# Attention heads of a two-layer kernel: order of splits and scores, two scales on ScalarE, residual reads one by one

## The chip, the cores and the metric

The kernel runs on one core of a Trainium2 chip. The metric is device time in microseconds (us) of one execution. Before the change it is 878.94 us, the median of 3 runs (876.65 to 882.01). The core's engines each work through a queue of their own, in program order: TensorE (PE in the profile) for matrix products, VectorE (DVE), ScalarE (ACT), GpSimd (POOL) and SyncE (SP); the last two, and ScalarE at the end, issue transfers. Engines wait for each other by semaphores.

## The reference

Two layers over a sequence of 512 tokens with 1024 features, all in float32. Layer 0 is a state-space mixer, layer 1 an attention with low-rank queries, keys and values (16 heads). The change lies in layer 1:

```python
def mla_mixer(u, positions, in_w, q_norm_w, kv_norm_w, uq_w, ukv_w, out_w):
    proj = u @ in_w                       # c_q 384, c_kv 256, k_r 64, z 2048
    q = (rms_norm(c_q, q_norm_w) @ uq_w)  # 16 heads x (128 + 64 rope)
    kv = (rms_norm(c_kv, kv_norm_w) @ ukv_w)  # 16 heads x (128 keys + 128 values)
    ...
    o = causal_block_attention(q_full, k_full, v, 192 ** -0.5)   # softmax over keys <= query
    o = o.reshape(bsz, seq, 2048) * jax.nn.silu(z)
    return o @ out_w
```

The layer's output is added to the residual stream `h`, and a last RMS norm gives the result.

## The kernel before

**Products in two halves.** To keep float32 accuracy, each operand is split into a rounded part and a remainder, both in the matmul's format: ScalarE casts the first (`whi`, `qh`, `ph`, `va`, `ah`), VectorE subtracts to get the second (`wlo`, `ql`, `pl`, `vb`, `al`). A product is then three matmuls per tile. Weights are loaded by GpSimd's queue into two raw buffers and split on the way (L303, L312).

**Heads.** The attention runs as one loop over 16 heads, `h`, with the work of different heads interleaved. While head `h` has its probabilities multiplied with the values (`product`), the scores of head `h + 1` are computed and turned into probabilities. Queries are taken in 4 blocks `b` of 128; block `b` sees `128 (b + 1)` keys. The steps are:

- `score(h, b)`: five matmuls into a PSUM bank (L871; block 0 is L874 to L876), on VectorE the mask and the row's maximum (L881, L883, called the reduction below), on ScalarE the exponential with its row sum (L257), on VectorE the reciprocal (L889), the scale by it (L890) and a transpose of 32x32 blocks (L892, tile `pb`), then four transfers on SP (L896) that write the block into a scratch tensor `pd` in main memory, so that keys and queries change places.
- `fetch(h)`: four reads on SP (L917), one for each block `kb` of 128 keys, of the turned probabilities into tiles `pl`.
- `turn(h, kb)`: ScalarE casts `pl` to `ph` (L924); VectorE subtracts, in place, so that `pl` is the remainder.
- `product(h, kb)`: three matmuls into the accumulator `po` of the head (L941): `ph` with both halves of the values, and `pl` with the first half. After block 3, VectorE multiplies with `silu(z)` (L943).

**What sets the order.** In this part the order on all engines is the program's own. `sched` runs a feed, a chain of generators that emit the large products and yield a cost in microseconds every six matmuls or so; each yield is a tick. Pieces are placed at a fraction of the feed's total cost, and fire at the first tick whose sum of costs has passed it. The fractions are module constants: `SC` for the four scores of head `h + 1` and its fetch, `TU` for the four turns, `PR` for the four products. An even head's feed is `front_a` (rope, queries and keys of the next pair's first head, cost 5.2) and one product `zgemm` for the gate z (5.2); an odd head's is `front_b` (5.9 with `front_v`, the values), and `zgemm`. From head 11 on, the steps of the output product `out_tok` take the place of `zgemm`. After heads 3, 7 and 11 ScalarE applies silu to four z tiles, which needs another function table before and after.

Work can also be put off: `defer(fn, lag)` puts a function on a list, and each tick counts its lag down; at zero it is emitted, in the order of the list. Before the change, the remainder `pl` has lag 1, the exponential lag 1, the finish of a score (reciprocal, scale, transpose, writes) lag 2, the rope's three VectorE instructions (L742 to L744) lag 3. A consumer that comes earlier calls `now()`. `fetch` calls it for all finishes of its head.

**The output product.** `out_tok(zt, 0, hd)` multiplies the first 8 heads with their weights, in steps of six matmuls for four token blocks `c`, two halves `n` of the features and four weight tiles `u`; four PSUM banks hold the sums of one `n`. The residual was written to the scratch tensor `hd` earlier and is read back into eight tiles `hr` that take the places of finished z tiles, in one go at `n = 0`, `u = 2`, which falls into head 13 (L1101). `done` (L1059) adds the sum.

Of the kernel before, what the change touches and what calls it, by code (L numbers as in the profile page):

```python
# [10 lines left out]
F32 = mybir.dt.float32  # L11
F32R = mybir.dt.float32r
AF = mybir.ActivationFunctionType
ALU = mybir.AluOpType

P = 128
T = 512
D = 1024
KD = D // P
NCH = T // P  # L20
# [20 lines left out]
GN = 16.84  # L41
G7 = 33.0
SF = (0.6, 1.0, 2.0, 3.2, 8.0)
SC = (0.0, 0.1, 0.18, 0.28, 0.55)
TU = (0.08, 0.17, 0.47, 0.57)
PR = (0.35, 0.45, 0.74, 0.94)
ZS = 0.8
KO = (4, 4, 4, 8, 10)
# [114 lines left out]
class Net:  # L163
# [527 lines left out]
    def mla(self):  # L691
        tc, nc, t, wk = self.tc, self.nc, self.t, self.wk
        v = nc.vector
# [6 lines left out]
        hd = self.dram.tile([NCH, P, D], F32, name="hd")  # L700
        turned = hd[:].rearrange("c (j a) d -> a (c j) d", a=32)
        vh, vl = [], []
        for k in range(KD):
            h = self.h[k]
            a = self.act.tile([P, T], F32R, tag="ah", name=self.nm("vh"))
            b = self.act.tile([P, T], F32R, tag="al", name=self.nm("vl"))
# [6 lines left out]
        for i in range(6):  # L713
# [6 lines left out]
            if i >= 2:  # L720
                for k in (2 * i - 4, 2 * i - 3):
                    ht = wk.tile([P, T], F32, tag="ph", name=self.nm("ht"))
                    v.transpose(ht[:], self.h[k][:])
                    for b in range(4):
                        m = slice(32 * b, 32 * b + 32)
# [3 lines left out]
            while pend and i >= NU:  # L729
                o = self.o16.tile([P, T], F32, tag="o", name=self.nm("cq"))  # L730
# [20 lines left out]
        def settle(f):  # L751
            for e in f["w"]:
                e.now()
            f["w"] = []
# [105 lines left out]
        def score(h, b):  # L860
            f, i = F[h // 2], h % 2
            settle(f)
            (qa, qb), kk = f["q", i], f["k", i]
            r = f["r", i]
            n = P * (b + 1)
            s = slice(b * P, (b + 1) * P)
            ps = self.bank("s")
            if b:
                seq = [(qa, kk[:, 0]), (qa, kk[:, 1]), (qb, kk[:, 0]), (r, k1), (r, k2)]
                for k, (x, y) in enumerate(seq):  # L870
                    nc.tensor.matmul(ps[:, :n], x[:, s], y[:, :n], start=k == 0, stop=k == 4)  # L871
            else:
                both = ps[:, :2 * P].rearrange("p (a t) -> p a t", a=2)
                nc.tensor.matmul(both, qa[:, s], kk[:, :, :P], start=True, stop=False)  # L874
                nc.tensor.matmul(ps[:, :P], qb[:, s], kk[:, 0, :P], start=False, stop=False)
                nc.tensor.matmul(both, r[:, s], k12[:, :, :P], start=False, stop=True)  # L876
            p = self.res.tile([P, n], F32, tag="res", name=self.nm("p"))
            st = wk.tile([P, 4], F32, tag="st", name=self.nm("st"), bufs=8)
            mask = self.mask[:, T - n:]
            if b == 0:  # L880
                v.tensor_tensor(p[:], ps[:, P:2 * P], mask, op=ALU.add)  # L881
                mask = p[:]
            v.tensor_tensor_reduce(p[:], ps[:, :n], mask, -SCALE, 3.0e38, ALU.add, ALU.min, st[:, 0:1])  # L883
            p_exp = self.defer(functools.partial(
                self.E, p[:], p[:], AF.Exp, scale=-1.0, bias=st[:, 0:1], accum_out=st[:, 1:2]))

            def finish():
                p_exp.now()
                v.reciprocal(st[:, 2:3], st[:, 1:2])  # L889
                v.tensor_scalar(p[:], p[:], st[:, 2:3], None, op0=ALU.mult)  # L890
                pb = wk.tile([P, T], F32, tag="pb", name=self.nm("pb"))
                v.transpose(pb[:, :n], p[:])  # L892
                turned = pd[h % 2][:].rearrange("(j a) q -> a j q", a=32)
                for i in range(4):
                    q = b * P + 32 * i
                    nc.sync.dma_start(turned[:, :n // 32, q:q + 32],  # L896
                                      pb[32 * i:32 * i + 32, :n].rearrange("a (j q) -> a j q", q=32))

            ends.append(self.defer(finish, 2))

        ends = []
        parts, acc = [[] for _ in range(MH)], {}
# [17 lines left out]
        def turn(h, kb):  # L920
            n = T - kb * P
            pl = back[h, kb]
            ph = wk.tile([P, T], F32R, tag="ph", name=self.nm("ph"))
            nc.scalar.copy(ph[:, :n], pl.bitcast(F32))  # L924
            e = self.defer(functools.partial(
                v.tensor_tensor, pl, pl.bitcast(F32), ph[:, :n].bitcast(F32), op=ALU.subtract))
            parts[h].append((ph, pl, e))

        def product(h, kb):
            f, i, n = F[h // 2], h % 2, T - kb * P  # L930
            if kb == 0:
                acc[h] = self.bank("po")
            po = acc[h]
            settle(f)
            ph, pl, e = parts[h][kb]
            e.now()
            va, vb = f["v"][kb // 2]
            s = slice((kb % 2) * 256 + i * P, (kb % 2) * 256 + (i + 1) * P)
            seq = [(va[:, s], ph[:, :n]), (vb[:, s], ph[:, :n]), (va[:, s], pl[:, :n])]
            for k, (x, y) in enumerate(seq):  # L940
                nc.tensor.matmul(po[:, kb * P:], x, y, start=kb == 0 and k == 0, stop=kb == NCH - 1 and k == 2)  # L941
            if kb == NCH - 1:
                v.tensor_tensor(zt[h][:], po[:], zt[h][:], op=ALU.mult)  # L943
# [25 lines left out]
        def steps(h):  # L969
            return [functools.partial(score, h, b) for b in range(NCH)] + [functools.partial(fetch, h)]  # L970
# [22 lines left out]
        with self.tc.manual_schedule(engines={E.SP, E.DVE, E.Activation, E.Pool}):  # L993
            self.lagging, self.look = True, 2
            self.sched(chain(front_b(0), front_v(0), zgemm(4)), list(zip(SF, steps(0))))
            for h in range(MH):
# [12 lines left out]
                if h % 2 and h < 14:  # L1009
                    feed.append(front_v(j))  # L1010
                at = SC if h + 1 < MH else ()
                pieces = [(x * cost, fn) for x, fn in zip(at, steps(h + 1))]
                pieces += [(x * cost, functools.partial(turn, h, b)) for b, x in enumerate(TU)]
                pieces += [(x * cost, functools.partial(product, h, b)) for b, x in enumerate(PR)]
# [18 lines left out]
    def out_tok(self, o, half, hd):  # L1033
        nc, wk, v, t = self.nc, self.wk, self.nc.vector, self.t
# [10 lines left out]
        def step(ps, c, w, n, ks, start, stop, a=0, b=T):  # L1045
            hi, lo = w
            s = slice(c * P, (c + 1) * P)
            seq = []
            for q, k in enumerate(ks):
                m = slice(q * T + a, q * T + b)  # L1050
                x, y, e = hl[k]
                e.now()
                seq += [(x[:, s], hi[:, m]), (y[:, s], hi[:, m]), (x[:, s], lo[:, m])]
            for i, (x, y) in enumerate(seq):
                nc.tensor.matmul(ps[:, a:b], x, y, start=start and i == 0, stop=stop and i == 5)  # L1055
# [29 lines left out]
        for n in range(2):  # L1085
            last = half == 1 and n == 1
            cuts = [(c, 0, T) for c in range(NCH)]
            if last:
                cuts[-1:] = [(NCH - 1, 0, T // 2), (NCH - 1, T // 2, T)]
            ps = [self.bank("ot") for _ in cuts]  # L1090
            base = U_OUT1 + 8 * half + 4 * n
            for u in range(2 if last else 4):
                w = self.weight("w", base + u)
                self.cut(o, half, 2 * u + 2 + OA)
                if half == 0 and n == 0 and u == 2:
                    for _, _, e in hl:
                        e.now()
                    for c in range(NCH):
                        r = [self.o16.tile([P, T], F32, tag="o", name=self.nm("hr")) for _ in range(2)]
                        for m in range(2):  # L1100
                            nc.sync.dma_start(r[m][:], hd[c, :, m * T:(m + 1) * T])  # L1101
                        self.hh.append(r)
                for q, (c, a, b) in zip(ps, cuts):
                    step(q, c, w, n, (2 * u, 2 * u + 1), u == 0, u == 3, a, b)
                    if b == T:
                        yield 1.3
                    if u == 3:
                        done(q, c, n)
                if half == 0 and n == 1:
                    self.cut(o, 1, 2 * u + 2)  # L1110
            if last:
                w2, w3 = self.weight("w", base + 2), self.weight("w", base + 3)
                for q, (c, a, b) in zip(ps, cuts):
                    step(q, c, w2, n, (4, 5), False, False, a, b)
                    step(q, c, w3, n, (6, 7), False, True, a, b)
                    done(q, c, n, a, b)
                    yield 2.6
# [77 lines left out]
```

## Time and profile before

| | us |
|---|---|
| median of 3 runs | 878.94 |
| the profiled execution | 880.34 |
| its span in the trace | 878.3 |
| TensorE busy | 823.3 (94%) |
| VectorE busy | 674.9 (77%) |
| ScalarE busy | 449.5 (51%) |
| first score to last product of the attention heads | about 480 to 822 |

A row of a timeline gives the start in us from the span's beginning, the length, the engine, the line, the instruction, what it writes and reads, its shape, and in brackets how long the engine sat idle before it and which instruction released it. A row of the waits gives who waited for whom, the total in us, how often, and the longest. A row of stretches gives the stretch, its length, busy time and count for PE, PEld (weight loads of TensorE), DVE, ACT and POOL, the clock granted to TensorE (1.00 is full speed), the DMA share and GB/s. A row of groups gives the number of instructions, their busy time in us and the mean in ns, then the idle time before them.

### The profile page before, as it was taken

To read this page: it belongs to the slowest core of one execution; us is meant where nothing else is said; L and a number is where in the kernel's file an instruction comes from. 1 tells how busy PE (TensorE), PEld (TensorE's weight loads), DVE (VectorE), ACT (ScalarE), POOL (GpSimd) and SP (SyncE) were. 2 spreads that over 40 slices of the span, in tenths; PEclk is the share of its full clock that TensorE was granted. 3 is DMA by queue.
4 is the path that set the end of the run, shared out by engine and by line. 5 is a ranking of instruction groups with operands and counts; after the bars stand their busy time and mean duration, and the time that the engine had idled before them with its cause. 6 is when DMAs were issued, how large, how long until landed. Compare 5 with 4: busy or idle time off the path is not lost.

```text
span 878.3 us, 11881 instructions
## 1 busy us (share of the span) xinstructions
PE 823.3 (94%) x4068; PEld 688.0 (78%) x4068; DVE 674.9 (77%) x1298; ACT 449.5 (51%) x794; POOL 50.5 (6%) x100
## 2 busy tenths in 40 slices
PE   7999999999999999999999979998988988878995
PEld 5887888888888888888887858786876877766885
DVE  7889898888888798775768867878786877856544
ACT  7566665646465565343535534464446456523333
POOL 0000000000000000000102110110101011000000
PEclk9999999999999999999999998998999999998998
DMA  6363542524333243236532455555555545475222
GB/s 226 110 189 109 166 144 97 167 73 145 104 128 128 97 144 96 108 98 142 141 100 61 115 128 130 154 138 123 133 132 138 147 115 130 127 226 133 72 72 96
DMA packets 144492, 111.57 MB, mean 127 GB/s; under 512 B 108592, under 2 KB 116272, under 8 KB 144432
## 3 DMA queue, kind: packets, MB, share of 16 engines
q1 hardware_dynamic: 134944, 79.61, 32.3%
q0 software_dynamic: 8768, 30.15, 11.6%
q10 hardware_dynamic: 720, 1.05, 0.3%
q8 instruction: 32, 0.52, 0.2%
q14 instruction: 28, 0.23, 0.1%
HBM read 93.60 MB, written 14.81 MB: 123 GB/s over the span
## 4 chain that ended last, share of the span: by engine, by line
PE 62%; DVE 16%; DMA 11%; SPq 4%; ACT 4%; issue 3%; DVEq 0%; POOL 0%; ACTq 0%
PE mm L332 41%; PE ot L1055 6%; DMA pd<-pb 5%; PE mm L341 4%; SPq L896 3%; DMA pl<-pd 3%; DVE wlo L63 2%; PE yd L149 2%; PE po L941 2%; DVE pb L892 1%; DVE p L890 1%; PE yd L332 1%; PE aux L141 1%; PE s L871 1%; PE aux L116 1%
## 5 line engine op out<-in xcount | busy, mean ns | idle before, releaser
L312 ACT CAST whi<-raw 128x1024 fp32r<-128x1024 f32 (+3 forms) x132 | 126.8, 965 | 194.0 <-PE mm L332 167.9
L63 DVE TENSOR_TENSOR wlo<-raw,whi 128x1024 fp32r<-128x1024 f32 (+3 forms) x132 | 146.4, 1113 | 42.2 <-ACT whi L312 42.1
L332 PE MATMUL mm<-ah,whi 128*128 128x512 f32 x384 | 153.8, 401 | 0.0
L332 PE MATMUL mm<-ah,wlo 128*128 128x512 f32 x384 | 150.1, 391 | 0.4 <-DVE wlo L63 0.4
L332 PE MATMUL mm<-al,whi 128*128 128x512 f32 x384 | 149.8, 390 | 0.0
L332 PE MATMUL mm<-vh,wlo 128*128 128x512 f32 x224 | 89.8, 401 | 1.2 <-DVE wlo L63 1.2
L332 PE MATMUL mm<-vh,whi 128*128 128x512 f32 x224 | 89.9, 401 | 0.6 <-ACT whi L312 0.6
L332 PE MATMUL mm<-vl,whi 128*128 128x512 f32 x224 | 89.1, 398 | 0.0
L332 PEld LDWEIGHTS mm<-ah,wlo 128*128 128x128 f32 x384 | 72.1, 188 | 16.1 <-DVE wlo L63 0.8
L332 PEld LDWEIGHTS mm<-ah,whi 128*128 128x128 f32 x384 | 72.1, 188 | 15.4 <-issue 1.4
L332 PEld LDWEIGHTS mm<-al,whi 128*128 128x128 f32 x384 | 72.2, 188 | 14.5 <-DVE al L353 0.3
L303 POOL DMA_DIRECT2D raw<-in_w_dram x36 | 19.2, 534 | 629.9 <-DMA hd<-ht 417.7
L924 ACT CAST ph<-pl 128x512 fp32r<-128x512 f32 (+1 forms) x64 | 27.8, 454 | 52.9 <-DMA pl<-pd 42.4
L1055 PE MATMUL ot<-whi,ah 128*128 128x512 f32 (+1 forms) x136 | 53.0, 389 | 0.0
L1055 PE MATMUL ot<-wlo,ah 128*128 128x512 f32 (+1 forms) x136 | 52.8, 388 | 0.0
L1055 PE MATMUL ot<-whi,al 128*128 128x512 f32 (+1 forms) x136 | 52.8, 388 | 0.0
L257 ACT ACTIVATE p<-p,st 128x128 f32<-128x128 f32 (+1 forms) x64 | 35.8, 560 | 32.7 <-DVE st L883 32.6
L332 PEld LDWEIGHTS mm<-vh,wlo 128*128 128x128 f32 x224 | 43.0, 192 | 11.7 <-DVE wlo L63 2.1
L332 PEld LDWEIGHTS mm<-vh,whi 128*128 128x128 f32 x224 | 43.0, 192 | 9.2 <-ACT whi L312 0.8
L63 DVE TENSOR_TENSOR pl<-pl,ph 128x512 fp32r<-128x512 f32 (+1 forms) x64 | 30.0, 481 | 25.7 <-ACT ph L924 25.7
L332 PEld LDWEIGHTS mm<-vl,whi 128*128 128x128 f32 x224 | 43.1, 192 | 8.1
L941 PE MATMUL po<-pl,va 128*128 128x512 f32 (+1 forms) x64 | 23.9, 374 | 24.3 <-DVE pl L63 24.3
(228 smaller groups left out, 1746.0 us busy)
## 6 DMA issues: line engine op xcount, KB each, us to landing
raw<-in_w_dram SPq DMA_DIRECT2D x64, 512.0 KB, 3.3
raw<-in_w_dram POOLq DMA_DIRECT2D x36, 512.0 KB, 3.7
L<-ac_d SPq DMA_DIRECT2D x32, 256.0 KB, 3.9
E<-ea_d SPq DMA_DIRECT2D x32, 128.0 KB, 3.4
raw<-in_ua_dram POOLq DMA_DIRECT2D x8, 512.0 KB, 3.9
pd<-pb SPq DMA_DIRECT2D x64, 64.0 KB, 2.0
pl<-pd SPq DMA_DIRECT2D x16, 256.0 KB, 2.7
pd<-pb SPq DMA_DIRECT2D x64, 48.0 KB, 1.8
```

The lines of the kernel that those rows point to most:

```text
L63: self.fn()
L116: nc.tensor.matmul(pp[c], self.BT[:, c * P:(c + 1) * P], flat(self.xw[:, c]), start=True, stop=True)
L149: nc.tensor.matmul(yd[64 * h:64 * h + 64, s], self.xdt[j][:, c, h, :], self.L[2 * j + h][:, s], start=True, stop=True)
L257: i = self.nc.scalar.activation(out, in_, func, **k)
L303: self.wqueue.dma_start(raw[:], self.t[kind][idx])
L312: nc.scalar.copy(hi[:, a:b], raw[:, a:b])
L332: self.nc.tensor.matmul(ps, a, b, start=i == 0, stop=i == len(seq) - 1)
L341: self.nc.tensor.matmul(p, seq[i][0], seq[i][1], start=i == 0, stop=i == 3 * ks - 1)
L896: nc.sync.dma_start(turned[:, :n // 32, q:q + 32], pb[32 * i:32 * i + 32, :n].rearrange("a (j q) -> a j q", q=32))
L924: nc.scalar.copy(ph[:, :n], pl.bitcast(F32))
L941: nc.tensor.matmul(po[:, kb * P:], x, y, start=kb == 0 and k == 0, stop=kb == NCH - 1 and k == 2)
L1055: nc.tensor.matmul(ps[:, a:b], x, y, start=start and i == 0, stop=stop and i == 5)
```

## The change

Five things are edited.

1. The fractions: scores at 0, 0.06, 0.14, 0.22 (before 0, 0.1, 0.18, 0.28), the fetch at 0.6 (0.55); turns at 0.18, 0.25, 0.46, 0.57 (before 0.08, 0.17, 0.47, 0.57).
2. `turn` emits the remainder `pl` at once behind the cast `ph`, instead of one tick later.
3. The finish of a score is cut in two: `even` (reciprocal and scale) with lag 2, and the transpose and writes with lag 3 for blocks 2 and 3, lag 2 for blocks 0 and 1.
4. For blocks 2 and 3 the scale is an activation (copy with a scale per partition) on ScalarE instead of VectorE's `tensor_scalar`.
5. The residual's eight reads are issued one by one ahead of the steps of `out_tok`: four in `n = 0`, `u = 2` (head 13), four in `n = 1`, `u = 0` (head 14).

```diff
-SC = (0.0, 0.1, 0.18, 0.28, 0.55)
-TU = (0.08, 0.17, 0.47, 0.57)
+SC = (0.0, 0.06, 0.14, 0.22, 0.6)
+TU = (0.18, 0.25, 0.46, 0.57)
...
-            def finish():
+            def even():
                 p_exp.now()
                 v.reciprocal(st[:, 2:3], st[:, 1:2])
-                v.tensor_scalar(p[:], p[:], st[:, 2:3], None, op0=ALU.mult)
+                if b > 1:
+                    nc.scalar.activation(p[:], p[:], AF.Copy, scale=st[:, 2:3])
+                else:
+                    v.tensor_scalar(p[:], p[:], st[:, 2:3], None, op0=ALU.mult)
+
+            p_even = self.defer(even, 2)
+
+            def finish():
+                p_even.now()
                 pb = wk.tile([P, T], F32, tag="pb", name=self.nm("pb"))
                 v.transpose(pb[:, :n], p[:])
...
-            ends.append(self.defer(finish, 2))
+            ends.append(self.defer(finish, 3 if b > 1 else 2))
...
             nc.scalar.copy(ph[:, :n], pl.bitcast(F32))
-            e = self.defer(functools.partial(
-                v.tensor_tensor, pl, pl.bitcast(F32), ph[:, :n].bitcast(F32), op=ALU.subtract))
-            parts[h].append((ph, pl, e))
+            v.tensor_tensor(pl, pl.bitcast(F32), ph[:, :n].bitcast(F32), op=ALU.subtract)
+            parts[h].append((ph, pl))
...
-                if half == 0 and n == 0 and u == 2:
+                fresh = half == 0 and u == (0 if n else 2)
+                if fresh:
                     for _, _, e in hl:
                         e.now()
-                    for c in range(NCH):
-                        r = [self.o16.tile([P, T], F32, tag="o", name=self.nm("hr")) for _ in range(2)]
-                        for m in range(2):
-                            nc.sync.dma_start(r[m][:], hd[c, :, m * T:(m + 1) * T])
-                        self.hh.append(r)
                 for q, (c, a, b) in zip(ps, cuts):
+                    if fresh:
+                        r = self.o16.tile([P, T], F32, tag="o", name=self.nm("hr"))
+                        nc.sync.dma_start(r[:], hd[c, :, n * T:(n + 1) * T])
+                        if n == 0:
+                            self.hh.append([])
+                        self.hh[c].append(r)
                     step(q, c, w, n, (2 * u, 2 * u + 1), u == 0, u == 3, a, b)
```

More of the change, by code (lines that the diff above doesn't have):

```diff
@@ L934, in product @@
             settle(f)
-            ph, pl, e = parts[h][kb]
-            e.now()
+            ph, pl = parts[h][kb]
             va, vb = f["v"][kb // 2]
```

## Prediction

> **What bounds the kernel now.** I read the page first, then TensorE's waits, the granted clock by stretches, and the timelines of a few heads. The page: TensorE (PE) is busy 94% of the span, so what can be won is mostly where it stands still:
>
> ```profile
> span 878.3 us, 11881 instructions
> PE 823.3 (94%) x4068; PEld 688.0 (78%) x4068; DVE 674.9 (77%) x1298; ACT 449.5 (51%) x794; POOL 50.5 (6%) x100
> ```
>
> The waits of PE between 480 and 822 us, the stretch of the attention heads (total, times, longest), hold nearly all of that:
>
> ```profile
> PE po L941 <- DVE pl L63: 24.3, 10, 4.6
> PE po L941 <- ACT ph L924: 9.2, 3, 5.0
> PE s L871 <- DVE vb L63: 2.9, 1, 2.9
> PE s L874 <- DVE k L63: 0.8, 1, 0.8
> PE mm L332 <- DVE wlo L63: 0.7, 1, 0.7
> ```
>
> Sum: 37.9 us. The first two rows, 33.5 us, are products (L941) that wait for the split of the probabilities: `ph` on ScalarE (ACT), `pl` on VectorE (DVE). A stall also costs afterwards. Two stalls from PE's timeline, and then the stretches (length, busy us of PE, PEld, DVE, ACT, POOL, then clock, DMA share, GB/s); 560 to 568 and 714 to 722 are those of the two stalls:
>
> ```profile
> 564.07 0.39 PE L941 MATMUL po<-pl,va 128*128 128x256 f32 x1 [2.02 <-DVE pl L63]
> ...
> 715.42 0.39 PE L941 MATMUL po<-pl,va 128*128 128x256 f32 x1 [2.27 <-DVE pl L63]
> ```
>
> ```profile
> 480.00:822.00 342.00, 303.90 (x1461) 256.32 (x1460) 252.77 (x585) 165.25 (x344) 40.17 (x77) 0.94 0.53 135
> 560.00:568.00 8.00, 5.98 (x32) 4.95 (x32) 6.24 (x10) 1.85 (x3) 0.54 (x1) 1.00 0.57 122
> 598.00:610.00 12.00, 8.75 (x33) 7.31 (x34) 8.53 (x18) 3.44 (x8) 1.07 (x2) 0.72 0.56 135
> 714.00:722.00 8.00, 6.58 (x28) 5.60 (x29) 5.43 (x11) 4.56 (x8) 0.00 (x0) 0.79 0.59 164
> 738.00:746.00 8.00, 5.37 (x21) 4.75 (x22) 4.50 (x14) 4.85 (x10) 1.40 (x3) 0.79 0.50 148
> ...
> 682.17:698.60 16.43, 16.43 (x93) 14.45 (x93) 15.34 (x36) 7.67 (x18) 1.60 (x3) 1.00 0.55 132
> ```
>
> 342 x (1 - 0.94) = 20.5 us of clock were withheld. Each patch takes 1.7 us (8 x 0.21) or 3.4 us (12 x 0.28); some 3 us of the sum fell into the stalls themselves, so 17.5 us come on top. The last row is head 9, which has no stall: 16.4 us, and a pair of heads at full pace takes about 32. **To be won at most: 37.9 + 17.5 = 55.4 us.**
>
> Why is `pl` late? ACT's largest wait of these 342 us, then head 6 in the timelines of DVE, ACT and PE (start, length, and in brackets the idle time before):
>
> ```profile
> ACT ph L924 <- DMA pl<-pd: 42.4, 10, 10.3
> ```
>
> ```profile
> 627.71 0.69 DVE L63 TENSOR_TENSOR pl<-pl,ph 128x512 fp32r<-128x512 f32 x1 [1.80 <-ACT ph L924]
> ...
> 636.27 1.18 DVE L63 TENSOR_TENSOR wlo<-raw,whi 128x1024 fp32r<-128x1024 f32 x1
> 637.38 0.68 DVE L742 TENSOR_TENSOR rraw<-rraw,con 128x512 f32<-128x512 f32 x1
> ...
> 639.30 0.62 DVE L63 TENSOR_TENSOR pl<-pl,ph 128x256 fp32r<-128x256 f32 x2
> ...
> 627.05 0.62 ACT L924 CAST ph<-pl 128x512 fp32r<-128x512 f32 x1 [3.46 <-DMA pl<-pd]
> 634.17 0.60 ACT L924 CAST ph<-pl 128x256 fp32r<-128x256 f32 x2
> ...
> 639.77 0.38 PE L941 MATMUL po<-pl,va 128*128 128x256 f32 x1 [3.04 <-DVE pl L63]
> ```
>
> `ph` of block 2 was ready at 634.5. Its `pl`, deferred by one tick, stood behind a weight's `wlo` and the rope (637.38 to 639.30, 1.92 us), and DVE worked without a gap: it was late, because ACT had sat 3.46 us on the first `ph` of the head, with the exponentials of the next head queued behind it.
>
> **The change, part by part.** In even heads the cost of the feed is 5.2 + 5.2 = 10.4, and pieces fire at the first tick past fraction x cost.
>
> (1) `pl` right behind `ph`. For block 2 it comes ahead of the rope: 1.92 us earlier. Nothing is added; but DVE now stops there if `ph` is late.
>
> (2) Turn 0 goes from the tick at 1.30 to that at 2.79. The exponentials of the next head's blocks 0 to 2 now stand ahead of `ph` 0, so ACT's 3.46 us and DVE's 1.80 us of idle are filled. Score 3 comes before the second half of the q gemm. The fetch (0.55 to 0.6) stays at the tick past 6.24, that is 6.88; it only has to stay behind the later finish.
>
> (3) Scale of blocks 2 and 3 on ACT:
>
> ```profile
> L890 DVE TENSOR_SCALAR p<-p,st 128x512 f32<-128x512 f32 x16 | 7.8, 487 | 0.6
> L890 DVE TENSOR_SCALAR p<-p,st 128x384 f32<-128x384 f32 x16 | 6.8, 427 | 0.6
> L1080 ACT ACTIVATE hr<-hr,ss x4: 722/724/725, 863.9 to 873.9; 128x512 f32<-128x512 f32 x4
> L251 ACT ACT_TABLE_LOAD  x12: 1283/1283/1283, 55.2 to 738.0; - x12
> ```
>
> DVE loses 0.49 + 0.43 = 0.91 us a head. L1080 is the same operation (copy with a scale per partition): 0.72 us for 512 columns; for 384 I take 0.62, between 0.43 (DVE's) and 0.72. L1080 ran beside exponentials, after the last table load at 738.0, so no load is added. ACT gains 1.34 us a head: 165 + 16 x 1.34 = 187 of 342 us, cover enough, but the scale is one more hand-over DVE - ACT - DVE ahead of the transpose.
>
> Together in head 6. Block 3's transpose ends where `wlo` starts, at 636.27; without 1.80 of idle and 0.91 of scales, and with 0.3 for ACT's hand-overs, at 633.9. `pl` 2 starts at 639.30 now; 1.80 + 0.91 + 1.92 = 4.6 us earlier is 634.7, and since block 3's exponential now waits behind block 2's scale (0.62) I put 0.7 on it: 635.4, done at 635.8. PE wants it at 639.77 - 3.04 = 636.7. **No stall, but a slack of only 0.9 us**; the longest stall of this kind, 4.6, is just covered too.
>
> Odd heads have no stall now; there `pl` 0 goes behind a k remainder and two reductions. Head 9:
>
> ```profile
> 686.23 0.69 DVE L63 TENSOR_TENSOR pl<-pl,ph 128x512 fp32r<-128x512 f32 x1
> ...
> 689.67 0.54 DVE L883 CUSTOM_DVE_ANT_0 p<-s,con 128x384 f32<-128x384 f32 x1
> ...
> 690.50 0.39 PE L941 MATMUL po<-pl,va 128*128 128x512 f32 x1
> ```
>
> Without `pl` the reduction starts at 689.1, `pl` follows and ends at 690.2: slack 0.3 us. Transposes 2 and 3 now come as a pair after `pl` 2, ending some 1 us later than now, and their eight writes fill SP's queue together, so the fetch goes some 1.7 us later; even heads want their `ph` 0 late enough to bear that by some 1.7 us.
>
> (4) The residual's reads. Eight reads stood between two pairs of head 14's writes (SP and the chain of waits), and both last heads stalled on the fetch:
>
> ```profile
> 770.96 3.95 SPq L1101 DMA_DIRECT2D hr<-hd  x8
> 773.41 6.03 DMA hr<-hd
> 789.62 0.79 PE L941 MATMUL po<-ph,va 128*128 128x512 f32 x1 [5.02 <-ACT ph L924]
> 810.63 0.50 PE L941 MATMUL po<-ph,va 128*128 128x512 f32 x1 [2.99 <-ACT ph L924]
> ```
>
> Three remain ahead of those writes, 3/8 of 6.03 = 2.3 us: 3.8 us earlier; also the exponentials of head 15 no longer queue behind `ph` of head 14. Of the other four, one goes ahead of head 15's last writes. I leave 1 us of the 5.02 and, with its clock, 3 us in head 15.
>
> **What stays of the 55.4 us.** The waits for k and wlo at the start, 1.5; head 0's first product, whose fetch isn't moved, 9.2 - 5.0 - 3.0 = 1.2; the tail, 4. After heads 3, 7 and 11 ACT loads tables for silu and DVE stands still:
>
> ```profile
> 587.16 0.69 DVE L63 TENSOR_TENSOR vb<-mm,va 128x512 fp32r<-128x512 f32 x1 [4.72 <-ACT va L852]
> ...
> 589.98 0.69 DVE L63 TENSOR_TENSOR pl<-pl,ph 128x512 fp32r<-128x512 f32 x1
> ...
> 591.21 0.39 PE L941 MATMUL po<-ph,va 128*128 128x512 f32 x1
> ```
>
> In head 4 the third reduction (0.54), its exponential (0.81), `ph` (0.62) and `pl` (0.69) now follow 589.98: `pl` at 592.8 where PE wants it at 591.7, and some 0.9 us again at block 2: 2 us each in heads 4 and 8, 4 together. Head 12's wait for `vb` (2.9 us, clock 1.2) hangs on the same silu and isn't touched: 4.1. The other eleven heads at 0.3, for slacks this thin: 3.3. Sum 18.1, gain 55.4 - 18.1 = 37.3 us. The profiled execution took 880.34 us (span 878.3, 2.0 around it), 1.4 above the median of 878.94: 880.3 - 37.3 - 1.4 = 841.6, **842 us**.
>
> One rule of the Trainium skill bears on the clock's part: "TensorE: Matmul & The Clock Gate", Part 1, has the clock halved only after a whole idle window of about 3.4 us. The trace differs: the stretch 714 to 722, clock 0.79, follows a stall of 2.27 us; the one with 1.00 followed 2.02 us. By the page head 12 and head 15 would keep 1 to 2 us less, 840 us; I go by the rows.
>
> **Rivals.** (a) The hand-over becomes the wait: `pl` 0, its slack 0.3 us in odd heads, or transpose 2 behind ACT's scale comes 1.5 us late in each of 15 heads, 22 us: 864 us. For it: ACT stands between two steps of DVE four times a head. Against it: ACT has the room.
> (b) The tail and heads 4, 8 and 12 come free too, since all before them is earlier: 842 - 12 = 830 us (4 + 4 + 4.1). Against it: the silu and its table loads stay where they are.
> (c) It doesn't do what it says: DVE, with 252.77 - 14.6 = 238 us of work in 305, cannot close its gaps, and each stall moves to the next remainder: 878 us.
> (d) Slower: the loop fetch - `ph` 0 - exponential 3 - transpose 3 - write - fetch becomes the bound. Landing, min/median/max, of the writes (L896) and of the fetch (L917):
>
> ```profile
> L896 SPq DMA_DIRECT2D pd<-pb x256: 302/449/1698, 496.9 to 800.5; - x128
> ...
> DMA to landing us min/median/max: 1.4/1.8/6.1
> ...
> DMA to landing us min/median/max: 2.5/3.0/4.2
> ```
>
> With the medians a lap of an even head is 6.1 us from `ph` 0 to the last transpose (627.8, behind the exponential of block 2, to 633.9 above), four issues of 0.45, 1.8 to land, an issue and 3.0 for the fetch: 13.1 us. In an odd head the `ph`, `pl`, reductions and `wlo` in front of two transposes make 7.2 us, and seven issues wait in a row: 15.6. Together 28.7, under PE's 32. At the maxima it is 28.7 + 2 x (4.3 + 1.2) = 39.7, or 7.7 over PE's 32 in each of 7 pairs: 842 + 54 = 896 us. It passes PE's pace once write and fetch together land 1.7 us late in each head, and the present time once they land some 4.3 us late. Against it: medians far below.
>
> **How the numbers follow.** Forecast 0.57 (832 to 853), (a) 0.17, (b) 0.12, (c) 0.06, (d) 0.08. Faster by over 0.5% (4.4 us, about what a measurement tells from no change): 0.57 + 0.17 + 0.12 = 0.86; same 0.06; slower 0.08. The range 828 to 868 leaves out (c), (d) and the ends of (a) and (b).
>
> **What would show it.** Right: in PE's waits `po <- pl` falls from 24.3 to under 5 us; the clock over the heads rises to 0.98; ACT's wait `ph <- DMA pl` drops from 42 us; the stall at head 14's first product is about 1 us; head 12's wait for `vb` stays. (a) shows as `po` waiting for `pl` or `ph` of 512 columns, (d) as ACT's `ph` waiting for the fetch in even heads, and (c) as DVE busy over 90% there. The forecast is wrong if waits of PE beyond 20 us remain between the first score and the last product.

## The result and the profile after

The changed kernel took **854.11 us** (median of 4 runs, 853.53 to 857.82) against 877.8 us of the kernel before beside it: ratio **0.973, 95% interval 0.969 to 0.978**. It is faster, as forecast, and inside the range (828 to 868), but the gain is 24 us where 37 were worked out. The profiled execution took 854.5 us, its span 852.5.

From the page after, the span and the busy times, with the instructions of each engine:

```profile
span 852.5 us, 11895 instructions
PE 815.8 (96%) x4068; PEld 678.7 (80%) x4068; DVE 660.1 (77%) x1266; ACT 468.6 (55%) x826; POOL 50.9 (6%) x100
```

DVE lost 32 instructions and ACT gained 32: the scales of two blocks in 16 heads. The waits of PE, and one of ACT's, between 480 and 822 us (total, times, longest):

```profile
PE po L947 <- DVE pl L933: 8.1, 17, 1.5
PE po L947 <- ACT ph L932: 8.0, 6, 3.9
PE s L871 <- DVE vb L63: 2.9, 1, 2.9
PE s L874 <- DVE k L63: 0.8, 1, 0.8
PE mm L332 <- DVE wlo L63: 0.7, 1, 0.7
...
ACT ph L932 <- DMA pl<-pd: 19.4, 9, 7.8
```

37.9 us of waits have become 20.5, but in 26 places instead of 16. ACT's wait for the fetch, 42.4 us before, was to go in the even heads; 19.4 us of it stay, 11.7 of them in heads 14 and 15. The granted clock, in the same stretch of 342 us and in the two places where it is still low (length, busy time of PE, PEld, DVE, ACT, POOL, then clock, DMA share, GB/s):

```profile
480.00:822.00 342.00, 321.03 (x1573) 267.44 (x1573) 249.04 (x570) 190.78 (x385) 43.00 (x82) 0.99 0.56 143
...
720.00:728.00 8.00, 6.51 (x20) 5.74 (x21) 4.89 (x17) 4.35 (x12) 2.59 (x5) 0.57 0.45 120
784.00:790.00 6.00, 5.18 (x15) 3.98 (x16) 4.20 (x7) 3.63 (x7) 0.53 (x1) 0.72 0.77 241
```

Withheld there: 8 x 0.43 = 3.4 us and 6 x 0.28 = 1.7 us, together 5.1. So 20.5 + 5.1 = **25.6 us stay of what the prediction put at 55.4; it had left 18.1.** In a second profile of the same kernel (run 11 below) the waits are 22.9 us. Five stalls from PE's timeline show which kinds are left (start, length, matmul, and in brackets how long PE stood still and for whom):

```profile
625.82 0.39 PE L947 MATMUL po<-pl,va 128*128 128x256 f32 x1 [0.79 <-DVE pl L933]
...
708.08 0.50 PE L947 MATMUL po<-pl,va 128*128 128x512 f32 x1 [1.52 <-DVE pl L933]
721.49 0.80 PE L871 MATMUL s<-k,qh 128*128 128x256 f32 x2 [2.94 <-DVE vb L63]
764.86 0.50 PE L947 MATMUL po<-ph,va 128*128 128x512 f32 x1 [1.70 <-ACT ph L932]
784.82 0.50 PE L947 MATMUL po<-ph,va 128*128 128x512 f32 x1 [3.93 <-ACT ph L932]
```

The first is head 6; heads 0, 2, 4, 8 and 10 stall at the same product by 0.79 or 0.80 us. Then head 11 at product 0, the wait for `vb` of head 12, and the first products of heads 14 and 15.

**Head 6, where the prediction had "no stall, but a slack of only 0.9 us".** SP's queue from the end of head 5 (start, time over which the transfers were issued, count), then the chain of waits over the same time (start, length, what; a `DMA` row runs from the start of the issue to the landing):

```profile
602.44 8.95 SPq L904 DMA_DIRECT2D pd<-pb  x9
```

```profile
609.20 1.67 SPq L904
...
610.90 4.12 DMA pd<-pb
615.09 2.96 DMA pl<-pd
```

The last of head 5's writes is out at 602.44 + 8.95 = 611.39, and the fetch has to wait until it has landed: 610.90 + 4.12 = 615.02, so it leaves at 615.09. The timelines of PE, ACT and DVE around it:

```profile
610.08 0.27 PE L947 MATMUL po<-pl,va 128*128 128x128 f32 x1
...
624.75 0.28 PE L947 MATMUL po<-ph,vb 128*128 128x256 f32 x1
...
618.13 0.62 ACT L932 CAST ph<-pl 128x512 fp32r<-128x512 f32 x1 [2.48 <-DMA pl<-pd]
...
605.32 0.43 DVE L933 TENSOR_TENSOR pl<-pl,ph 128x256 fp32r<-128x256 f32 x1 [1.53 <-ACT ph L932]
605.66 1.16 DVE L900 STREAM_TRANSPOSE pb<-p 128x384 f32<-128x384 f32 x2
...
618.78 0.69 DVE L933 TENSOR_TENSOR pl<-pl,ph 128x512 fp32r<-128x512 f32 x1 [2.22 <-ACT ph L932]
...
624.20 1.23 DVE L63 TENSOR_TENSOR wlo<-raw,whi 128x1024 fp32r<-128x1024 f32 x1 [0.22 <-ACT whi L312]
```

The pair of transposes stands behind `pl` 2 of head 5, for which DVE waited 1.53 us: its `ph` stood on ACT behind the two scales (603.76 to 604.99). The fetch leaves 5.0 us after head 5's last matmul (610.08). Before, that matmul started at 622.36 and the fetch left 1.6 us behind it (timelines of SP, DVE and PE):

```profile
611.11 9.56 SPq L896 DMA_DIRECT2D pd<-pb  x16
623.97 1.86 SPq L917 DMA_DIRECT2D pl<-pd  x4
...
617.01 0.71 DVE L892 STREAM_TRANSPOSE pb<-p 128x512 f32<-128x512 f32 x1
...
622.36 0.27 PE L941 MATMUL po<-pl,va 128*128 128x128 f32 x1
```

So DVE still stands 2.22 us idle on the first `ph`, as before (1.80), although three exponentials now go ahead of it, and `pl` 2 is late again, behind a weight's `wlo`, though only by 0.79 us instead of 3.04.

### The profile page after: what moved, and what is told of

Its sections match the earlier page's. It is cut to its first block, busy times and chain, and to the rows that moved or that the text cites. A ratio compares the mean times of both kernels' runs of the same rounds, so it can differ in the third digit from the quotient of the medians.

```text
span 852.5 us, 11895 instructions
## 1 busy us (share of the span) xinstructions
PE 815.8 (96%) x4068; PEld 678.7 (80%) x4068; DVE 660.1 (77%) x1266; ACT 468.6 (55%) x826; POOL 50.9 (6%) x100
## 3 DMA queue, kind: packets, MB, share of 16 engines
q0 software_dynamic: 8768, 30.15, 11.7%
## 4 chain that ended last, share of the span: by engine, by line
PE 62%; DVE 13%; DMA 10%; ACT 7%; issue 4%; SPq 4%; DVEq 0%; POOL 0%; ACTq 0%
PE mm L332 40%; PE ot L1061 7%; DMA pd<-pb 4%; PE mm L341 4%; DMA pl<-pd 3%; SPq L904 3%; PE yd L149 2%; DVE wlo L63 2%; PE s L871 2%; ACT whi L312 2%; PE yd L332 1%; PE aux L141 1%; DVE pl L933 1%; PE po L947 1%; PE aux L116 1%
## 5 line engine op out<-in xcount | busy, mean ns | idle before, releaser
L332 PE MATMUL mm<-vh,wlo 128*128 128x512 f32 x224 | 87.7, 392 | 1.2 <-DVE wlo L63 1.2
L332 PE MATMUL mm<-vl,whi 128*128 128x512 f32 x224 | 87.3, 390 | 0.0
L332 PE MATMUL mm<-ch,whi 128*128 128x512 f32 x104 | 42.1, 405 | 0.0
L332 PE MATMUL mm<-cl,whi 128*128 128x512 f32 x104 | 41.3, 397 | 0.0
```

What stands on the lines that cost most here:

```text
L332: self.nc.tensor.matmul(ps, a, b, start=i == 0, stop=i == len(seq) - 1)
```

## The experiments

The first four are each one part of the change on the kernel before; the cut of the finish with its later lag and the scale on ScalarE count as one part, and no run separates them.

**1. The remainder alone.**

```diff
-            e = self.defer(functools.partial(v.tensor_tensor, pl, ...))
+            v.tensor_tensor(pl, pl.bitcast(F32), ph[:, :n].bitcast(F32), op=ALU.subtract)
```

> The kernel before with one edit: the remainder pl is emitted at once behind its cast ph. Theory A (the rope was the wait): pl 2 of each even head comes 1.92 us earlier on VectorE, so the nine stalls shrink from 24.3 us to about 9, with two or three patches of slow clock fewer: 860 us. Theory B (ScalarE, blocked on the fetch, was the wait): turn 0 still stands ahead of the next head's exponentials, VectorE now waits for ph sooner, and what the rope gives back is lost there: 872 us or more.

Measured: 871.3 us, ratio 0.996 (0.993 to 0.998). From the waits of PE and of ACT:

```profile
PE po L939 <- DVE pl L925: 15.7, 13, 2.7
PE po L939 <- ACT ph L924: 11.5, 5, 6.1
...
ACT ph L924 <- DMA pl<-pd: 65.7, 14, 10.2
```

`po` waits less for `pl`, and more for `ph`; ACT's wait for the fetch grows from 42.4 to 65.7 us. The remainder was not late by its place in the queue alone.

**2. The order alone.**

```diff
-SC = (0.0, 0.1, 0.18, 0.28, 0.55)
-TU = (0.08, 0.17, 0.47, 0.57)
+SC = (0.0, 0.06, 0.14, 0.22, 0.6)
+TU = (0.18, 0.25, 0.46, 0.57)
```

> The kernel before with the new fractions alone (scores, fetch and turns). Theory A: pl 2 still stands behind the rope, so the stalls of even heads stay near 2 us each: 868 us. Theory B: ScalarE and VectorE no longer idle on the first ph (3.5 and 1.8 us a head), and most of the gain of the whole change is here: 860 us or less.

Measured: 872.5 us, ratio 0.994 (0.992 to 0.997). Waits of PE and ACT, and a stall from PE's timeline:

```profile
PE po L941 <- DVE pl L63: 27.6, 18, 4.7
...
ACT ph L924 <- DMA pl<-pd: 5.3, 2, 4.4
```

```profile
554.98 0.50 PE L941 MATMUL po<-pl,va 128*128 128x512 f32 x1 [1.74 <-DVE pl L63]
```

The later turns do what the second part of the change was to do: ACT's wait for the fetch falls to 5.3 us. Yet ACT now stands 31.6 us at the same casts until PE's products release it (1.8 us before), and with `pl` still one tick behind `ph`, `po` now waits for `pl` at product 0 too (554.98). Neither theory had that.

**3 and 4. The scale on ScalarE alone, and the residual's reads one by one alone.**

```diff
-                v.tensor_scalar(p[:], p[:], st[:, 2:3], None, op0=ALU.mult)
+                if b > 1:
+                    nc.scalar.activation(p[:], p[:], AF.Copy, scale=st[:, 2:3])
...
+            p_even = self.defer(even, 2)
...
-            ends.append(self.defer(finish, 2))
+            ends.append(self.defer(finish, 3 if b > 1 else 2))
```

```diff
-                if half == 0 and n == 0 and u == 2:
+                fresh = half == 0 and u == (0 if n else 2)
...
```

> The kernel before with the finish cut in two and the scale of blocks 2 and 3 on ScalarE alone. Relief of VectorE (0.91 us a head) would give about 5 us: 873 us. The rival, the lap through memory: transposes 2 and 3 come one tick later, so the writes and the fetch come later and ScalarE sits longer on the first ph: no gain, 878 to 890 us.

> The kernel before with the residual's reads one by one alone. If the eight reads held up head 14's writes: the stall there falls from 5.0 to 1 or 2 us and loses a patch of slow clock: 873 us. If head 14's fetch was late by its scores anyway: 878 us.

Measured: 878.4 us, ratio 1.000 (0.997 to 1.002), and 877.5 us, ratio 1.000 (0.998 to 1.003). With the scale on ACT, ACT's wait for the fetch is 56.9 us instead of 42.4; with the single reads head 14's stall is 2.07 us instead of 5.02, as wanted, but the waits for `pl` are 27.9 us instead of 24.3. By itself neither part can be told from no change. The four parts alone add up to 11 us (6.4 + 5.3 - 0.7 + 0.3 = 11.3); the whole change gave 24.

**5. The changed kernel without the scale on ScalarE** (scale on VectorE, lag 2, as before).

> The changed kernel with the scale of blocks 2 and 3 back on VectorE and one finish of lag 2: order, pl and reads together. Theory A (order and pl open the way together, VectorE's relief of 0.91 us a head still counts, since even heads stall 0.8 us at pl 2 in the changed kernel): each even head loses 0.9 us more, 862 us. Theory B (the pair of transposes in odd heads and the hand-over to ScalarE cost what the relief brings, as the scale alone gave nothing): 852 to 856 us, with the fetch of even heads some 2 us earlier in the head.

Measured: 851.2 us, ratio 0.970 (0.966 to 0.974): not slower than the changed kernel; the 3 us by which it is faster are not clear of noise, since the intervals overlap. The end of head 14 in SP's timeline and the first product of head 15, here and then in the changed kernel:

```profile
766.61 8.10 SPq L896 DMA_DIRECT2D pd<-pb  x16
...
778.27 1.80 SPq L917 DMA_DIRECT2D pl<-pd  x4
...
781.68 0.50 PE L939 MATMUL po<-ph,va 128*128 128x512 f32 x1
```

```profile
772.64 5.16 SPq L904 DMA_DIRECT2D pd<-pb  x8
780.57 2.01 SPq L925 DMA_DIRECT2D pl<-pd  x4
```

Without the scale on ACT the last writes are out at 774.71, the fetch of head 15 leaves at 778.27 and its product doesn't wait; with it the last eight writes are out at 777.80, the fetch leaves at 780.57, and PE waits 3.93 us. That isn't all gain: in kernel 5 head 14 stalls 2.19 and 1.55 us (1.70 and 0.55 in the changed kernel), so the last two heads together wait 3.7 us instead of 6.2. And head 4 stalls 2.37 us at `pl` 2 instead of 0.80: there the relief of VectorE was worth something. All waits of PE between 480 and 822 us are 19.8 us, against 20.5 and, in run 11, 22.9.

**6. The scale on ScalarE only where it is emitted in even heads** (that is, for the scores of odd heads; lag 2 for the others).

```diff
-                if b > 1:
+                if b > 1 and h % 2:
...
-            ends.append(self.defer(finish, 3 if b > 1 else 2))
+            ends.append(self.defer(finish, 3 if b > 1 and h % 2 else 2))
```

> The changed kernel with ScalarE's scale and lag 3 kept in even heads only; in odd heads blocks 2 and 3 are finished as before (VectorE, lag 2), ahead of pl 2. If the lap through memory makes the stalls of 0.8 + 0.2 us in even heads (ScalarE waits 2.5 us for the fetch there, whose writes came as a pair late in the odd head), the fetch comes 1 to 2 us earlier, these stalls vanish, and the time is 846 us. If VectorE's work is the cause: odd heads get 0.91 us more, 855 to 858 us.

Measured: 851.2 us, ratio 0.969 (0.966 to 0.973). Head 6 in the timelines of SP, PE, ACT, DVE and PE:

```profile
604.45 4.15 SPq L904 DMA_DIRECT2D pd<-pb  x8
612.21 1.77 SPq L925 DMA_DIRECT2D pl<-pd  x4
...
609.77 0.27 PE L947 MATMUL po<-pl,va 128*128 128x128 f32 x1
...
615.24 1.02 ACT L932 CAST ph<-pl 128x512 fp32r<-128x512 f32 x2
...
616.17 0.65 DVE L933 TENSOR_TENSOR pl<-pl,ph 128x512 fp32r<-128x512 f32 x1
...
623.83 0.28 PE L947 MATMUL po<-ph,vb 128*128 128x256 f32 x1
623.95 0.28 PE L947 MATMUL po<-pl,va 128*128 128x256 f32 x1
```

Here the odd head's writes end at 608.6, the fetch leaves 2.4 us after head 5's last matmul instead of 5.0, neither ACT nor DVE waits for it, and the 0.79 us at `pl` 2 are gone, in heads 2 and 10 too. What the loop emits in head 6 is the same in both kernels; only head 5's part differs. And kernels 5 and 9, which also finish head 6's scores on VectorE, have the fetch at +1.5 and +2.3 us and no stall at `pl` 2 of head 6. **That the late fetch makes this stall is shown**, for head 6 best; head 2's is no steady sign (0.25 us in run 11, 0.84 in kernel 5). Head 15, whose scores still have their scale on ACT, keeps its stall (3.94 us). That the scale in the even heads helps is not shown: with it (851.15) and without it (851.21) the time is the same. The 846 us expected were not reached: heads 0, 4, 8, 11, 12 and 14 keep stalls of about the old size.

**7 and 8. The silu in heads 4, 8 and 12** instead of 3, 7 and 11, on the changed kernel and on kernel 6.

```diff
-                if h < 13 and h % 4 == 3:
-                    pieces.append((ZS * cost, functools.partial(zsilu, h // 4 + 1)))
+                if h in (4, 8, 12):
+                    pieces.append((ZS * cost, functools.partial(zsilu, h // 4)))
```

> The changed kernel with the three groups of silu one head later, in heads 4, 8 and 12 instead of 3, 7 and 11, where no value's remainder waits behind them. If head 12's wait for vb (2.9 us, and 3.4 us of clock) and the 0.75 us at the first products of heads 4 and 8 hang on the silu's place on ScalarE: 8 us less, 846 us. If ScalarE's 4.8 us only hit the next head's exponentials instead: 852 to 856 us, with stalls in heads 5, 9 and 13.

> The two edits before this one together. If both causes hold and are independent: 838 to 840 us, all that my forecast left out for even heads and head 12. If they share the same slack: no better than the better one of them.

Measured: 861.2 us, ratio 0.981 (0.978 to 0.985), and 854.8 us, ratio 0.975 (0.971 to 0.979): each slower than the same kernel with the silu in its old place, by 5 to 7 us on the changed kernel (its intervals just touch) and by 3.7 us on kernel 6. A stall of kernel 7 from PE's timeline, in head 5, where the changed kernel has none:

```profile
601.11 0.50 PE L947 MATMUL po<-ph,va 128*128 128x512 f32 x1 [1.59 <-ACT ph L932]
```

The wait for `vb` (2.9 us) is gone. In its place heads 5 and 9 wait 1.6 and 1.5 us each at product 0, a score waits 1.9 us at 748.74, and all waits of PE grow from 20.5 to 23.2 us.

**9 and 11. The order and the remainder together on the kernel before** (edits 1 and 2), and beside it the changed kernel once more.

> The kernel before with two parts of the change, pl right behind ph and the new order; the scale stays with VectorE and the eight reads stay together. Alone these two gave 6.5 us (871.3 against 877.7) and 5.4 us (872.5). Theory A: they only work together, because the new order brings the wait of pl at product 0 (which lagged one tick behind the remainders) and pl alone leaves ScalarE's wait on the fetch (65.7 us); together they carry all but the last two heads: 851 to 855 us, pl waits near 11 us as in the run without the scale, and the stall of head 14's first product back at 3 to 5 us. Theory B: the single reads carry a part of their own (alone they were worth nothing, since the stall of head 14 was then taken by pl): 857 to 861 us, with 4 us or more in heads 14 and 15 alone.

> The changed kernel itself, beside the other two on one chip: 852 to 856 us. Theory A (the two parts order and pl carry the gain): within 2 us of e9_order_and_pl. Theory B (the reads carry a part, the scale none): 3 us or more below it.

Measured: 857.2 us, ratio 0.976 (0.973 to 0.979), and 856.3 us, ratio 0.976 (0.973 to 0.979). **Two of the four parts together give as much as the whole change; alone they gave 6.4 and 5.3 us, together 21.** The other two together are worth 0.9 us, which can't be told from nothing. But it need not be nothing twice. Kernel 5 is kernel 9 with the single reads, and its ratio, 0.970, is lower. First product of head 14 in PE's timeline, and the stretch of the last heads, of kernel 9:

```profile
770.88 0.79 PE L939 MATMUL po<-ph,va 128*128 128x512 f32 x1 [6.31 <-ACT ph L924]
```

```profile
757.00:797.00 40.00, 32.63 (x140) 26.32 (x140) 20.90 (x45) 13.54 (x27) 2.11 (x4) 0.87 0.60 173
```

and of kernel 5:

```profile
763.50 0.50 PE L939 MATMUL po<-ph,va 128*128 128x512 f32 x1 [2.19 <-ACT ph L924]
```

```profile
757.00:797.00 40.00, 36.17 (x156) 28.83 (x155) 25.09 (x53) 15.31 (x29) 2.64 (x5) 0.96 0.56 169
```

The stall is 4.1 us shorter and the clock withholds 40 x 0.09 = 3.6 us less: by the medians the reads are worth some 6 us (857.2 to 851.2), and the scale on ACT then takes 3 to 5 of them back (851.2 to 854.1 or 856.3). Kernels 5 and 9 were not run side by side, and the intervals just touch or overlap, so these two sizes are not shown; of the traces' part the shorter stall is firm, the clock less so (last section).

**10 and 12. The silu at the end of heads 3, 7 and 11**, behind both casts of `va`, on kernel 6 and on kernel 5.

```diff
-                    pieces.append((ZS * cost, functools.partial(zsilu, h // 4 + 1)))
+                    pieces.append((2 * cost, functools.partial(zsilu, h // 4 + 1)))
```

> The changed kernel with ScalarE's scale only in even heads (851.2 us before) and with the silu of heads 3, 7 and 11 put at the end of these heads, behind both casts of va, so that VectorE's vb no longer waits for the silu and its table loads. Theory A: the wait for vb at head 12 (2.9 us, and 3.4 us of withheld clock behind it) goes, and the first exponentials of the next head bear the silu's 4.8 us: 845 to 847 us, and the VectorE wait for va falls from 18.5 us to under 8. Theory B: the silu then stands ahead of the first exponentials and the first ph of heads 4, 8 and 12, and product 0 of these heads is late instead, by 2 to 3 us each: 853 to 858 us, as when the silu was put into even heads (861.2).

> The changed kernel with the scale back on VectorE in all heads (851.2 us before) and the silu of heads 3, 7 and 11 at the end of these heads. Theory A: the silu's new place is worth about 1 us, as in the even-heads version (851.2 to 850.3), since the wait for vb (2.9 us) is replaced by one for a rotated half of the rope on ScalarE (2.5 us): 849 to 851 us. Theory B: with fewer hand-overs in front of head 12 the second wait hides too: 845 to 848 us.

Measured: 850.3 us, ratio 0.969 (0.966 to 0.972), and 850.1 us, ratio 0.969 (0.965 to 0.972). From PE's waits of kernel 12:

```profile
PE mm L332 <- ACT rraw L790: 2.5, 1, 2.5
```

The row for `vb` (2.9) is gone, and one for `rraw`, which ACT copies behind the silu, has come (2.5). The silu only changes which wait it makes. These two are the fastest kernels of the study, 4 to 6 us below the changed one, but not to be told from kernels 5 and 6.

## Why the prediction was right, and where it was not

**The direction and the mechanism were right.** Products waited for the split of the probabilities because ACT sat on the fetch and `pl` stood at the end of DVE's queue; `po <- pl` fell from 24.3 to 8.1 us, the clock over the heads rose from 0.94 to 0.99. That the first two parts need each other (the turns fill the idle time, but bring a wait at product 0 unless `pl` moves up) was in neither the sum nor a rival; kernels 1, 2 and 9 show it. That the gain came out at 24 of 37 us and still inside the range is owed to the width of the range, not to the sum.

**By its own test it stands on the edge**: it named waits above 20 us between the first score and the last product as the sign of being wrong. 20.5 remain in the stretch in which it counted its 37.9, 19.0 without the two waits up to the first score, and 22.9 and 21.4 in run 11. `po <- pl` was to be under 5 us and is 8.1. Term by term, forecast against measured:

- Start: 1.5, measured 1.5 (0.8 + 0.7). Head 0: 1.2, measured 1.9 (0.87 at product 0, 0.79 and 0.20 at products 2 and 3). Heads 4 and 8: 2 each; the trace has 0.56 and 0.8 in each, and shorter ones of 0.2: a little less than forecast.
- **Head 12, `vb`: 2.9 was right (2.94); its clock was put at 1.2 and cost 3.4.** That size is chance: in run 11 the same stall of the same kernel cost no clock at all (last section).
- **Tail: 1 for head 14 was 1.70, and another 0.55 at later products; 3 for head 15 were 3.93 and 1.7 of clock.** 4 forecast, 7.9 measured, the largest miss of the sum. The step that failed is part 4's: it took the fetch of head 15 to be held by one read only, and didn't count that part 3 puts off the last eight writes (kernel 5: without it no stall in head 15, though head 14 waits 1.5 us more).
- **"Other eleven heads at 0.3 each", 3.3 us: measured 4.5, and in another shape**: 0.98 (0.79 and 0.19) in each of heads 2, 6 and 10, 1.52 in head 11, in the rest almost nothing.

**The other step that failed is in parts 2 and 3, head 6: that DVE's 1.80 us of idle are filled, that "a slack of only 0.9 us" is left, and that even heads can bear a fetch some 1.7 us later.** The prediction saw the cause itself (two transposes as a pair, eight writes in a row) and sized it at 1.7 us. Against head 5's last matmul the fetch moved from +1.6 to +5.0, 3.4 us, and the 1.80 weren't won but became 2.22. The last transpose ends 1.4 us later (before at 617.72, after at 606.82, that is 4.6 and 3.3 us ahead of the last matmul); the writes then take 4.6 us to be issued where they took 3.0, one issue alone 1.67; and the fetch leaves 3.7 us after the last write's issue has ended (611.39 to 615.09), where the lap reckoned with the median landing of 1.8. Before, it was already 3.3 (620.67 to 623.97). This is rival (d), in a small form: the loop through memory isn't the bound, but it used up the slack on which the forecast stood. Kernel 6 shows it, since with the fetch at +2.4 the stall is gone. Kernel 9, with the order and `pl` alone, has it at +2.3: of the 3.4 us, 0.7 come with the first two parts and 2.7 with part 3. Whether it is the scale on ACT or the lag of 3 that does it stays open, as no run has one without the other. The sum for head 6 also left out a wait of 0.85 us of DVE, ahead of the transpose of block 2 at 633.86, for earlier writes out of `pb` to land; in the changed kernel it is 0.34.

**The scale on ACT was taken for a relief of DVE by 0.91 us a head.** The operation cost what was worked out (groups by form, busy time and mean in ns):

```profile
L891 ACT ACTIVATE p<-p,st 128x512 f32<-128x512 f32 x16 | 11.5, 716 | 1.5 <-DVE st L889 1.5
L891 ACT ACTIVATE p<-p,st 128x384 f32<-128x384 f32 x16 | 9.9, 617 | 15.2 <-DVE st L889 15.1
```

0.72 and 0.62 us, as forecast, and no table load was added (12, as before). But ACT also stood 15.2 us ahead of it waiting for DVE's reciprocal, 15.2 / 16 = 0.95 us for block 2, where 0.3 us had been allowed for head 6's hand-overs. And the relief brought little: kernels 5 and 12, without it, are not slower. What it saves in head 4 (2.37 us down to 0.80) it loses again in heads 6, 10 and 15.

**The rivals.** (a) did come, but in one head: 1.52 us at `pl` 0 of head 11, not 1.5 us in fifteen. (b) is out: the silu's stalls stay, and kernels 7, 8, 10 and 12 only move them. (c) is out: DVE is busy 73% there. (d) as above.

**What stays open.** 55.4 - 25.6 = 29.8 us should have come off the span; 25.8 did. A part of the other 4 lies in what a stall costs beyond its row: at head 6 the matmuls start at 624.75 and 625.82, 1.07 us apart, where two of them follow each other by 0.12 (kernel 6: 623.83 to 623.95), so 0.95 is lost where the row says 0.79. If each of the ten stalls more than before costs as much, that is 10 x 0.16 = 1.6 us, an estimate from this one stall. The rest of 2.4 is hardly more than the rounding of the mean clock: 0.005 of 342 us are 1.7 us, in the 20.5 us of clock from which the 55.4 were added up.

## What to carry to other kernels

When two engines wait for each other around a loop through memory, a deferred step and the order of the pieces have to be moved together: each alone gave a quarter to a third of what both gave. Size the loop by the last write ahead of the read, from the end of its issue to the read's (3.3 us before, 2.7 to 3.7 us in kernels 5, 6, 9 and the changed one, at head 6), not by the median landing of all writes (1.8 us). And before work is moved to an idler engine, ask at which steps the one it leaves is late; here the relief saved 1.6 us in head 4 and little elsewhere, and the added hand-over and the later writes took that back.

## What the runs showed of the hardware

The clock's reaction to a stall isn't set by the stall's length alone, nor by the kernel. The wait for `vb` of 2.94 us was followed by 3.4 withheld us in the changed kernel (720 to 728 at 0.57, above). In run 11, the same kernel again, the same stall was followed by none:

```profile
721.94 0.51 PE L871 MATMUL s<-k,qh 128*128 128x256 f32 x2 [2.94 <-DVE vb L63]
```

```profile
720.00:728.00 8.00, 6.06 (x30) 5.14 (x31) 6.31 (x20) 5.17 (x13) 2.59 (x5) 1.00 0.57 136
```

Kernel 6 has the stall too, ending at 718.27, and the clock stays at 1.00 from 716 to 728. A stretch of kernel 6 was slowed although no stall just ahead of it is above 0.8 us; ahead of it PE stood still for 0.73 and 0.79 us, 1.5 of the 4 us up to 590:

```profile
590.00:600.00 10.00, 10.00 (x45) 8.53 (x44) 8.74 (x23) 5.41 (x12) 0.67 (x2) 0.83 0.66 188
```

The Trainium skill, "TensorE: Matmul & The Clock Gate", Part 1, has the clock halved after at least one idle window of about 3.4 us. The 2.94 us of run 11 and of kernel 6 agree with it, and so do the 3.93 us ahead of head 15 (784 to 790 at 0.72); the 2.94 us of the changed kernel's first profile and the stretch from 590 to 600 don't. So the clock's share of such a forecast can be off by some 3 us for a stall of this length, and two profiles of one kernel can differ by as much.
